# The residual of a layer's last norm in two rounded parts, added by TensorE for seven blocks, and renewals of states spread over more steps

## The chip, the cores and the metric

The kernel runs on one core of one Trainium2 chip. The metric is the device time of one execution in microseconds (us), the median of several runs. Every time in this document comes from such runs or from the hardware profile of one execution. The engines are called PE (TensorE), DVE (VectorE), ACT (ScalarE), POOL (GpSimd) and SP (SyncE, which here only issues DMAs); each runs its own instructions in the order in which they were written into its queue, and waits on semaphores for the others.

## The reference

One inference step of one decoder layer, for 256 tokens of a prompt and 8 sequences of 8 sampled tokens: 320 tokens, model width 2048, all in f32. Cut to what matters here:

```python
def conv_ffn(h, conv_state, w_up, conv_w, conv_b, w_down):
    up = h @ w_up
    up, new_conv = causal_depthwise_conv(up, conv_state, conv_w, conv_b)
    g, u = jnp.split(up, 2, axis=-1)
    return (jax.nn.gelu(g, approximate=True) * u) @ w_down, new_conv

def decoder_layer(x, ssm_state, ssm_conv_state, ffn_conv_state, p):
    ...
    mix = jnp.concatenate([gate_out, ssm_out], axis=-1) @ p["w_out"]
    x = x + rms_norm(mix, p["norm_mix_post"])
    f, new_ffn_conv = conv_ffn(rms_norm(x, p["norm_ffn_pre"]), ffn_conv_state, ...)
    x = x + rms_norm(f, p["norm_ffn_post"])
    return x, new_ssm, new_ssm_conv, new_ffn_conv, chunk_v
```

`ssm_out` comes from a state-space recurrence. Its state of each sampled sequence, 4 groups of heads by 8 sequences, is carried forward: new state = old state times a total decay + (inputs times decays) @ B. The kernel calls this a renewal. It returns the new states, and `y`, the last `x`.

## The kernel before

Everything is kept transposed: the 2048 channels are 16 blocks of 128 partitions, and a block's free axis holds the 320 tokens. Weights are the stationary operand, 128x128; the tokens move, 128x320. To keep f32's accuracy at a faster rate, each f32 operand is split in two parts of the format f32r (a rounded f32): x = hi + lo. A product is three matmuls: hi·hi, hi·lo, lo·hi.

**Slabs.** Weights come in slabs of 512 KB, eight 128x128 blocks (`slab`, from L119): SP loads `wraw`, ACT casts it to `whi` (L130), DVE subtracts to get `wlo` (L132). There are three buffers of each. `accumulate` (L143 to L145) issues the three matmuls of a block, so a slab is 24 of them. All slabs' instructions have a raised priority in the scheduler that writes each engine's order.

**Projections.** `project` runs an up-projection for 512 output columns in 8 slabs: six that hold two input blocks for all four output blocks (input blocks 0 to 11), then two that hold the input blocks 12 to 15 for two output blocks each. `chunk_out` runs one chunk of a down-projection in 8 slabs; DVE adds each result to `acc` (L236). After each slab, `tick` lets a background task of the list `bg` take one step.

**FFN.** 11 groups of 512 columns of each half. `ffn_up(g)` runs two `project` calls (the gate's half, then the other half) from `hT[0]`, `hT[1]` (the two parts of the normed input), with the convolution, GELU and product behind them; `split` (L370 ACT, L371 DVE) makes two parts of the product. `chunk_out` of group g is written after `ffn_up(g + 1)`.

**Renewals.** The background task there is `renewals` (first two steps for the prompt's states, then 4 groups of heads by 2 halves of the sequences, eight batches). For a group ACT copies and DVE scales tokens into `xb_parts` (L1191, L1194); for each of the batch's four states POOL multiplies `st` by the decay (L1199), PE makes `up_ps` (L1211), DVE adds it (L1213), ACT stores the state. SP loads states (L1171) and tokens (L1180) between slabs of weights. A step is a `yield`; the task has 105 of them.

**Tail.** After the last chunk: sums of squares over channels on PE (`token_sums`, L284), the reciprocal root on DVE and ACT, and `spread` (L292), which makes of the root a 128x320 tile in PSUM; ACT copies it to `r4s` for POOL, which doesn't read PSUM here. Then for each of the 16 blocks y = acc · root + x1, where x1 is the residual (in the tile `acc_mix`), and a store of y. `hand_over` (L1244) brings x1 into PSUM (`x1p`) by an f32 matmul with the identity, for blocks 0 to 10. Three engines do the blocks:

- `by_pe` (0 to 3): DVE multiplies, PE adds `acc` into the same PSUM tile by an f32 matmul with the identity (L1281), ACT copies the sum out (L1282) and ACT's queue stores it.
- `whole` (4 to 10): DVE multiplies (`timed`, L1271) and adds x1p (L1276); SP's queue stores (L1248).
- `by_pool` (11 to 15): POOL multiplies (L1271) and adds x1 itself (L1288); SP's queue stores.

`after` and `behind` chain each engine's instructions of the tail in the order in which the calls are written.

Of the kernel before, what the change touches and what calls it, by code (L numbers as in the profile page):

```python
# [34 lines left out]
def hybrid_step(  # L35
# [29 lines left out]
    with tc.high_priority(offset=300000):  # L65
        dve.memset(ones, 1.0)

        ps = misc("early")
        for _ in range(EARLY):
            pe.matmul(ps[:, :P], ones, ones, start=True, stop=True)  # L70
    upper = cp.tile([P, P], F32, name="upper")
    later = cp.tile([P, P], F32, name="later")
    bd2 = cp.tile([P, P], F32, name="bd2")
# [3 lines left out]
    bd = bd2[:NS, :NS]  # L77

    def masks():
        make_upper_triangular(nc, upper, 1.0, diag=True)  # L80
        make_lower_triangular(nc, later, 1.0, diag=False)
        pool.memset(bd2, 0.0)
        for op, fill, base in ((ALU.is_gt, 1.0, 1 - TS), (ALU.is_ge, 0.0, 0)):
            pool.affine_select(out=bd2, in_=bd2, pattern=[[-TS, P // TS], [0, TS]], compare_op=op, fill=fill, base=base,
                               channel_multiplier=1)

        d4 = ident.rearrange("p (i r t) -> p i r t", r=4, t=TS)
        dve.tensor_reduce(out=low[:, 0:1], in_=d4[:, :, 2:4], axis=mybir.AxisListType.XYZ, op=ALU.add)
        d5 = ident.rearrange("p (i k t) -> p i k t", k=2, t=TS)
        dve.tensor_reduce(out=low[:, 1:2], in_=d5[:, :, 1], axis=mybir.AxisListType.XY, op=ALU.add)  # L90
        dve.tensor_scalar(out=low, in0=low, scalar1=-1.0, scalar2=None, op0=ALU.mult)
        for r in range(2):
            rs = slice(64 * r, 64 * r + 64)
            dve.tensor_tensor(out=upper_s[rs], in0=upper[rs, rs], in1=bd2[rs, rs], op=ALU.mult)
        pool.memset(cmask, 1.0)
        cm4 = cmask.rearrange("p (h b) i -> p h b i", h=2)
        pool.affine_select(out=cm4, in_=cm4, pattern=[[0, 2], [-8, 4], [1, 32]],
                           compare_op=ALU.is_ge, fill=0.0, base=0, channel_multiplier=0)
        pool.affine_select(out=cm4, in_=cm4, pattern=[[0, 2], [8, 4], [-1, 32]],
                           compare_op=ALU.is_ge, fill=0.0, base=7, channel_multiplier=0)  # L100
# [63 lines left out]
    def finish(task):  # L164
        while task in bg:
            tick()
# [896 lines left out]
    with tc.tile_pool(name="fp", bufs=1) as fp:  # L1063
# [91 lines left out]
        def renewals():  # L1155

            raw = hp.tile([P, 4, NT], F32R, tag="ohi", name="xb").bitcast(F32).rearrange("p k n -> p (k n)").rearrange("p (h c) -> p h c", h=2)
            part = hp.tile([P, 4, NT], F32R, tag="olo", name="xb_parts").rearrange("p k n -> p (k n)").rearrange("p (h c) -> p h c", h=2)
            tote = fp.tile([P, NH, NB], F32, name="tote")
            for g, s1, x1d, _ in rest:  # L1160
                yield from repeat(None, 2)
                with tc.issue_after(rsqrt_ins[-1]):
                    dve.tensor_tensor(out=s1, in0=s1, in1=x1d, op=ALU.add)
                act.dma_start(o_ssm_p[g], s1)

            def load(g, h):

                st = [fp.tile([P, 512], F32, tag="st", name="st", bufs=4) if h == 0 else
                      cp.tile([P, 512], F32, tag=("s1", "x1d")[i % 2], name="st", bufs=3) for i in range(4)]
                for i in range(4):  # L1170
                    sp.dma_start(st[i], state_ssm[4 * h + i, g])  # L1171
                return st

            def tokens(g):

                rows = xb_d[g].rearrange("(h i t) c -> i t h c", h=2, i=4)
                for i in range(4):
                    for r in range(4):
                        at = 32 * i + TS * r
                        sp.dma_start(raw[at:at + TS], rows[i])  # L1180

            with tc.issue_after(slab_load[-1]):
                sp.dma_start(tote, tote_d)
                ahead = [load(0, 0)]
            yield
            with tc.issue_after(slab_load[-1]):
                tokens(0)
            for g in range(4):
                h0 = 8 * g
                yield from repeat(None, 3)  # L1190
                act.copy(part, raw)  # L1191
                yield
                for at, m in ((slice(0, 512), 0), (slice(512, 640), 1)):
                    dve.scalar_tensor_tensor(out=part[:, :, at], in0=part[:, :, at].bitcast(F32), scalar=low[:, m:m + 1], in1=raw[:, :, at],  # L1194
                                             op0=ALU.mult, op1=ALU.add)
                for h in range(2):
                    st = ahead.pop(0)
                    for i in range(4):
                        pool.tensor_tensor(out=by_head(st[i]), in0=by_head(st[i]),  # L1199
                                           in1=tote[:, h0:h0 + 8, 4 * h + i:4 * h + i + 1].to_broadcast([P, 8, 64]), op=ALU.mult)  # L1200
                        yield
                    if h == 0:
                        ahead.append(load(g, 1))
                    elif g < 3:
                        ahead.append(load(g + 1, 0))
                        tokens(g + 1)
                    yield from repeat(None, 2)
                    grown = [misc("up_ps") for _ in range(4)]
                    for i in range(4):
                        at = slice(32 * i, 32 * i + 32)  # L1210
                        pe.matmul(grown[i], part[at, h, 512:], part[at, h, :512], start=True, stop=True, tile_position=(32 * i, 0))  # L1211
                    for i in range(4):
                        dve.tensor_tensor(out=st[i], in0=st[i], in1=grown[i], op=ALU.add)  # L1213
                        yield
                        act.dma_start(o_ssm_s[4 * h + i, g], st[i])

        NG = NF // 4
        nxt = ffn_up(0)
        grow = renewals()
        bg.append(grow)  # L1220
        for g in range(NG):
            hi, lo = nxt
            if g < NG - 1:
                nxt = ffn_up(g + 1)
            if g == 0:
                acc = fp.tile([P, KD, NT], F32, name="acc_ffn")
            if g == NG - 1:
                finish(grow)
            chunk_out(ffn_w_down, g, hi, lo, g == 0, last if g == NG - 1 else None)

        act.dma_start(o_fconv_p, ptf)
# [5 lines left out]
        def after(engine):  # L1237
            return tc.issue_after(behind[engine]) if engine in behind else nullcontext()

        def hand_over(*blocks, where=banks):  # L1240
            for nb in blocks:
                x1p[nb] = where[0].tile([P, 512], F32, tag=where[1], name="x1p")[:, :NT]
                with after(pe):
                    behind[pe] = pe.matmul(x1p[nb], ident, x1[:, nb, :], start=True, stop=nb > 3).ins  # L1244

        def stored(queue, k, n):
            with after(queue):
# [3 lines left out]
        with after(pe):  # L1251
            sums = token_sums(sq4, more=True)
        behind[pe] = sums_ins[-1]
        hand_over(0)
        with after(pe):
            sums = token_sums(one[0], sums)
        r = rsqrt_by_root(sums, 1.0 / D)
        behind[pe] = sums_ins[-1]
        hand_over(4, 5)
        with after(pe):  # L1260
            r4 = spread(r)
        behind[pe] = spread_ins[-1]
# [5 lines left out]
        def timed(engine, k, n, root):  # L1268
            f = acc[:, k:k + n, :]
            with after(engine):  # L1270
                behind[engine] = engine.tensor_tensor(out=f, in0=f, in1=root.unsqueeze(1).to_broadcast([P, n, NT]), op=ALU.mult).ins  # L1271

        def whole(k, n):
            timed(dve, k, n, r4)
            for nb in range(k, k + n):
                behind[dve] = dve.tensor_tensor(out=acc[:, nb, :], in0=acc[:, nb, :], in1=x1p[nb], op=ALU.add).ins  # L1276
            stored(sp, k, n)
# [7 lines left out]
        def by_pool(k, n):  # L1285
            timed(pool, k, n, r4s)
            with after(pool):
                behind[pool] = pool.tensor_tensor(out=acc[:, k:k + n, :], in0=acc[:, k:k + n, :], in1=x1[:, k:k + n, :], op=ALU.add).ins  # L1288
            stored(sp, k, n)

        timed(dve, 0, 1, r4)
        hand_over(1)
        by_pe(0)
        whole(4, 2)
        hand_over(6, 7, where=more)
        timed(dve, 1, 1, r4)
        by_pe(1)
        by_pool(12, 2)
        whole(6, 2)
        hand_over(2, 8)  # L1300
        timed(dve, 2, 1, r4)
        by_pe(2)
        hand_over(9, 3)
        timed(dve, 3, 1, r4)
        by_pe(3)
        whole(8, 2)
        by_pool(14, 2)
        hand_over(10)
        whole(10, 1)
        by_pool(11, 1)  # L1310


_OUTS = [
# [81 lines left out]
```

## Time and profile before

| | |
|---|---|
| median of 3 runs | 1760.93 us (1760.37 to 1761.53) |
| profiled execution | 1762.04 us |
| its span in the profile | 1760.3 us |
| outside the span | 1.74 us |
| DMA, whole span | 301.38 MB, mean 171 GB/s |
| renewals in the trace | from 938.08 (first xb_parts) on |
| last projection matmul starts, first of the sums of squares starts | 1743.54 us, 1743.76 us |

How to read it: an engine's busy time is a sum over its instructions, and engines overlap. In rows of groups, the source line and engine stand ahead of operation, output <- inputs, shapes and count; behind the bar stand the busy time in us and the mean of one in ns, then the engine's idle time ahead of these instructions and what ended it. In a timeline, start and duration in us come first, and brackets hold the idle time just before and its releaser. In the chain of waits, each row is a piece of the path that ended last. Matmuls are pipelined: one's recorded duration is longer than the distance to the next.

### The profile page before, as it was taken

The page shows a single profiled execution, that of the slowest core. Times are in us where ns is not written, and L with a number is a line of the kernel's source. Part 1 is how long each engine was busy: PE and PEld are TensorE (multiplying, and loading weights), DVE is VectorE, ACT ScalarE, POOL GpSimd, SP SyncE. Part 2 cuts the span into 40 slices and gives each one's busy share as a digit, 9 for nine tenths or more (in the row PEclk, how much of TensorE's full clock was granted, in tenths as well). Part 3 has the DMA queues.
Part 4 walks back from the last instruction along what each step waited for, and adds up shares of the span by engine and source line. Part 5 has one row for each costly group of instructions (what it writes and reads, how often), then busy time and mean ns, then how long its engine had stood idle before and what let it go on. Part 6 is the DMA issues. An engine that isn't in the chain of part 4 may idle for free.

```text
span 1760.3 us, 31124 instructions
## 1 busy us (share of the span) xinstructions
PE 1751.6 (100%) x12178; PEld 1729.8 (98%) x12178; DVE 1154.1 (66%) x1949; ACT 806.6 (46%) x1172; POOL 272.7 (15%) x588
## 2 busy tenths in 40 slices
PE   9999999999999999999999999999999999999998
PEld 9999999999999999999999999999999999999997
DVE  7449754656767576668966677676657565656575
ACT  7344545333854445545544434343434343333335
POOL 1003200000111101021331212130201010111004
PEclk9999999999999999999999999999999999999999
DMA  7466655456665644554756666756454545454542
GB/s 248 144 167 182 185 151 150 153 155 190 216 206 163 201 145 131 166 161 143 228 169 223 189 217 195 222 185 192 151 153 148 156 148 155 148 155 147 155 151 104
DMA packets 228179, 301.38 MB, mean 171 GB/s; under 512 B 19936, under 2 KB 150848, under 8 KB 227840
## 3 DMA queue, kind: packets, MB, share of 16 engines
q1 hardware_dynamic: 215856, 281.27, 52.4%
q10 hardware_dynamic: 10640, 13.60, 2.2%
q0 software_dynamic: 1536, 4.52, 1.0%
q8 instruction: 96, 1.57, 0.4%
q14 instruction: 51, 0.42, 0.1%
HBM read 283.47 MB, written 15.61 MB: 170 GB/s over the span
## 4 chain that ended last, share of the span: by engine, by line
PE 95%; DVE 2%; DMA 1%; ACT 0%; POOL 0%; issue 0%; SPq 0%; POOLq 0%; DVEq 0%; ACTq 0%
PE ps L143 20%; PE ps L145 20%; PE ps L144 20%; PE pd L143 10%; PE pd L144 10%; PE pd L145 10%; PE y_ps L900 1%; DMA wraw<-in_ffn_w_up 1%; DVE wlo L132 1%; PE yo_ps L848 0%; PE sg L705 0%; PE tsum L284 0%; DVE h_lo L374 0%; DVE acc_mix L1042 0%; DMA vt<-in_xT 0%; ACT whi L130 0%
## 5 line engine op out<-in xcount | busy, mean ns | idle before, releaser
L132 DVE TENSOR_TENSOR wlo<-wraw,whi 128x1024 fp32r<-128x1024 f32 x470 | 582.9, 1241 | 436.9 <-ACT whi L130 434.9
L130 ACT CAST whi<-wraw 128x1024 fp32r<-128x1024 f32 x470 | 492.0, 1047 | 730.3 <-PE ps L144 437.7
L143 PE MATMUL ps<-h_hi,whi 128*128 128x320 f32 x2528 | 782.1, 310 | 0.4 <-ACT whi L130 0.4
L144 PE MATMUL ps<-h_lo,whi 128*128 128x320 f32 x2528 | 779.8, 309 | 0.0
L145 PE MATMUL ps<-h_hi,wlo 128*128 128x320 f32 x2528 | 777.8, 309 | 0.0
L143 PEld LDWEIGHTS ps<-h_hi,whi 128*128 128x128 f32 x2528 | 474.8, 188 | 4.2 <-issue 2.3
L144 PEld LDWEIGHTS ps<-h_lo,whi 128*128 128x128 f32 x2528 | 475.1, 188 | 0.0
L145 PEld LDWEIGHTS ps<-h_hi,wlo 128*128 128x128 f32 x2528 | 474.4, 188 | 0.1
L143 PE MATMUL pd<-fhi,whi 128*128 128x320 f32 x704 | 217.2, 309 | 0.0
L144 PE MATMUL pd<-flo,whi 128*128 128x320 f32 x704 | 217.0, 308 | 0.0
L145 PE MATMUL pd<-fhi,wlo 128*128 128x320 f32 x704 | 216.9, 308 | 0.0
L143 PE MATMUL pd<-ohi,whi 128*128 128x320 f32 x448 | 139.5, 312 | 0.0
L145 PE MATMUL pd<-ohi,wlo 128*128 128x320 f32 x448 | 138.5, 309 | 0.0
L144 PE MATMUL pd<-olo,whi 128*128 128x320 f32 x448 | 138.5, 309 | 0.0
L143 PEld LDWEIGHTS pd<-fhi,whi 128*128 128x128 f32 x704 | 132.2, 188 | 0.7 <-issue 0.7
L144 PEld LDWEIGHTS pd<-flo,whi 128*128 128x128 f32 x704 | 132.2, 188 | 0.2 <-issue 0.2
L145 PEld LDWEIGHTS pd<-fhi,wlo 128*128 128x128 f32 x704 | 132.2, 188 | 0.0
L1099 POOL COPY ptf<-pad 128x2 f32<-128x2 f32 x88 | 24.2, 275 | 508.3 <-DVE pad L1087 507.5
L236 DVE TENSOR_TENSOR acc_ffn<-acc_ffn,pd 128x320 f32<-128x320 f32 x160 | 77.2, 482 | 34.5 <-PE pd L145 33.6
L143 PEld LDWEIGHTS pd<-ohi,whi 128*128 128x128 f32 x448 | 84.0, 188 | 1.4 <-issue 0.7
L144 PEld LDWEIGHTS pd<-olo,whi 128*128 128x128 f32 x448 | 84.1, 188 | 0.2 <-issue 0.2
L145 PEld LDWEIGHTS pd<-ohi,wlo 128*128 128x128 f32 x448 | 84.1, 188 | 0.0
(301 smaller groups left out, 1513.6 us busy)
## 6 DMA issues: line engine op xcount, KB each, us to landing
wraw<-in_ffn_w_up SPq DMA_DIRECT2D x176, 512.0 KB
wraw<-in_w_in SPq DMA_DIRECT2D x142, 512.0 KB
wraw<-in_ffn_w_down SPq DMA_DIRECT2D x88, 512.0 KB
wraw<-in_w_out SPq DMA_DIRECT2D x64, 512.0 KB
st<-in_state_ssm SPq DMA_DIRECT2D x64, 256.0 KB
out_ssm_state_sample<-st ACTq DMA_DIRECT2D x32, 256.0 KB
cs<-dacs_d SPq DMA_DIRECT2D x16, 320.0 KB
xr<-in_xT SPq DMA_DIRECT2D x4, 640.0 KB
```

Of the source, the lines that this page charges most:

```text
L130: act.copy(hi[:, :m], raw[:, :m])
L132: dve.tensor_tensor(out=lo[:, :m], in0=raw[:, :m], in1=hi[:, :m].bitcast(F32), op=ALU.subtract)
L143: pe.matmul(ps, whi, xhi, start=first, stop=False)
L144: pe.matmul(ps, whi, xlo, start=False, stop=False)
L145: newest[0] = pe.matmul(ps, wlo, xhi, start=False, stop=last).ins
L236: dve.tensor_tensor(out=acc[:, nb, :], in0=acc[:, nb, :], in1=ps[:, :NT], op=ALU.add)
L900: pe.matmul(ps[64 * i:64 * i + 64, cols], w(hl), x(hl, m, cpx), tile_position=(0, 64 * i), **flags)
L1099: pool.tensor_copy(ptf[:, k, :], pad[:, 256:258])
```

## The change

Line numbers of the changed kernel are 1 to 19 higher. It does five things:

- Twelve blocks of the residual x1 (0 to 11) are split in two f32r parts, one block a step, as a background task after the renewals. The parts go into `hT[0]` and `hT[1]`, the buffers of the FFN's normed input, each block once the last up-projection has read it for the last time. `finish(grow)` moves one group up, so that the renewals end before.
- `hand_over` makes x1p from these parts with two f32r matmuls (with `ident_r`, an f32r identity that POOL makes among the masks at the kernel's start) in place of one f32 matmul, and for blocks 0 to 11 in place of 0 to 10.
- PE adds seven blocks (0 to 3 and 8, 9, 10) in place of four; DVE adds 4 to 7 and 11; POOL keeps 12 to 15 and gives 11 away. DVE multiplies 2 and 3, 8 and 9, 10 and 11 as pairs.
- So ACT's queue stores seven times and SP's five times, in place of four and seven.
- The renewals take more steps: four before the tokens, twelve in place of three ahead of the first group's parts, and two in place of one behind each of POOL's multiplications: 150 steps.

```diff
+    ident_r = cp.tile([P, P], F32R, name="ident_r")
...
     def masks():
+        pool.tensor_copy(ident_r, ident)
...
                 act.dma_start(o_ssm_p[g], s1)
+            yield from repeat(None, 4)
...
-                yield from repeat(None, 3)
+                yield from repeat(None, 3 if g else 12)
...
                                            in1=tote[:, h0:h0 + 8, 4 * h + i:4 * h + i + 1].to_broadcast([P, 8, 64]), op=ALU.mult)
+                        yield
                         yield
...
+        def x1_parts():
+
+            for nb in range(12):
+                split(hT[0][:, nb, :], hT[1][:, nb, :], x1[:, nb, :])
+                yield
+
...
+            if g == NG - 2:
+                finish(grow)
+                parted = x1_parts()
+                bg.append(parted)
             if g == 0:
                 acc = fp.tile([P, KD, NT], F32, name="acc_ffn")
-            if g == NG - 1:
-                finish(grow)
...
+        added = (0, 1, 2, 3, 8, 9, 10)
...
-                with after(pe):
-                    behind[pe] = pe.matmul(x1p[nb], ident, x1[:, nb, :], start=True, stop=nb > 3).ins
+                for i in range(2):
+                    with after(pe):
+                        behind[pe] = pe.matmul(x1p[nb], ident_r, hT[i][:, nb, :], start=i == 0, stop=i == 1 and nb not in added).ins
...
-        hand_over(0)
+        hand_over(0, 1)
...
         hand_over(4, 5)
+        hand_over(6, where=more)
...
         def whole(k, n):
-            timed(dve, k, n, r4)
+            if n:
+                timed(dve, k, n, r4)
+            n = max(n, 1)
...
         timed(dve, 0, 1, r4)
-        hand_over(1)
         by_pe(0)
         whole(4, 2)
-        hand_over(6, 7, where=more)
+        hand_over(7, where=more)
         timed(dve, 1, 1, r4)
         by_pe(1)
         by_pool(12, 2)
         whole(6, 2)
-        hand_over(2, 8)
-        timed(dve, 2, 1, r4)
+        hand_over(2, 3)
+        timed(dve, 2, 2, r4)
         by_pe(2)
-        hand_over(9, 3)
-        timed(dve, 3, 1, r4)
         by_pe(3)
-        whole(8, 2)
+        hand_over(8, 9)
+        timed(dve, 8, 2, r4)
+        by_pe(8)
+        by_pe(9)
         by_pool(14, 2)
-        hand_over(10)
-        whole(10, 1)
-        by_pool(11, 1)
+        hand_over(10, 11)
+        timed(dve, 10, 2, r4)
+        by_pe(10)
+        whole(11, 0)
```

Where this moves instructions, at three places. The first is VectorE at the first renewal. `wlo` is the low half of a slab, its number the slab's; `xb_parts` is what the renewal's matmuls read. Before:

```order
L132 TENSOR_TENSOR wlo_10398<-wraw_10394,whi_10396 128x1024
L132 TENSOR_TENSOR wlo_10434<-wraw_10430,whi_10432 128x1024
L1194 TENSOR_SCALAR xb_parts_9596<-xb_parts_9596,low_91,xb_9595 128x2x512
L1194 TENSOR_SCALAR xb_parts_9596<-xb_parts_9596,low_91,xb_9595 128x2x128
L132 TENSOR_TENSOR wlo_10469<-wraw_10465,whi_10467 128x1024
```

and PE there, which takes the renewal's four matmuls in the middle of the slab whose high half is `whi_10396`:

```order
L145 MATMUL pd_0_10_10400<-fhi_9299,wlo_10398 128x320
L143 MATMUL pd_0_10_10400<-fhi_9299,whi_10396 128x320
L1211 MATMUL up_ps_10277<-xb_parts_9596 128x512
L1211 MATMUL up_ps_10278<-xb_parts_9596 128x512
L1211 MATMUL up_ps_10279<-xb_parts_9596 128x512
L1211 MATMUL up_ps_10280<-xb_parts_9596 128x512
L144 MATMUL pd_0_10_10400<-flo_9300,whi_10396 128x320
```

VectorE after the change:

```order
L134 TENSOR_TENSOR wlo_10547<-wraw_10543,whi_10545 128x1024
L1197 TENSOR_SCALAR xb_parts_9598<-xb_parts_9598,low_92,xb_9597 128x2x512
L1197 TENSOR_SCALAR xb_parts_9598<-xb_parts_9598,low_92,xb_9597 128x2x128
L134 TENSOR_TENSOR wlo_10578<-wraw_10574,whi_10576 128x1024
L134 TENSOR_TENSOR wlo_10608<-wraw_10604,whi_10606 128x1024
L134 TENSOR_TENSOR wlo_10639<-wraw_10635,whi_10637 128x1024
L134 TENSOR_TENSOR wlo_10669<-wraw_10665,whi_10667 128x1024
L134 TENSOR_TENSOR wlo_10722<-wraw_10718,whi_10720 128x1024
L134 TENSOR_TENSOR wlo_10778<-wraw_10774,whi_10776 128x1024
```

and PE's renewal matmuls, now at the end of the slab of `wlo_10846`, whose low half VectorE makes second after the last of the rows above:

```order
L146 MATMUL ps_6656_3_10773<-h_lo_104,whi_10844 128x320
L147 MATMUL ps_6656_3_10773<-h_hi_103,wlo_10846 128x320
L1215 MATMUL up_ps_10872<-xb_parts_9598 128x512
L1215 MATMUL up_ps_10873<-xb_parts_9598 128x512
L1215 MATMUL up_ps_10874<-xb_parts_9598 128x512
L1215 MATMUL up_ps_10875<-xb_parts_9598 128x512
L145 MATMUL ps_6656_0_10770<-h_hi_103,whi_10883 128x320
```

Before, VectorE made the parts behind the low half of the slab that PE needs next, while PE was already in the slab (`10396`) in which it asks for them; now the parts stand eight low halves ahead of the end of the slab in which PE asks.

The second place is ACT in the second half of the last up-projection, `ffn_up(10)`: `whi` is a slab's high half, `gcv` the gate's convolution, `h_hi` the buffer that takes x1's high part (`acc_mix` holds x1). Before:

```order
L1143 DMA out_ffn_conv_sample<-stg_17761 128x64
L130 COPY whi_18149<-wraw_18147 128x1024
L1101 ACTIVATE gcv_17762<-gcv_17762 128x336 x2
L130 COPY whi_18179<-wraw_18177 128x1024
L130 COPY whi_18209<-wraw_18207 128x1024
L130 COPY whi_18239<-wraw_18237 128x1024
```

After:

```order
L1145 DMA out_ffn_conv_sample<-stg_17763 128x64
L372 COPY h_hi_103<-acc_mix_106 128x320
L132 COPY whi_18151<-wraw_18149 128x1024
L1103 ACTIVATE gcv_17764<-gcv_17764 128x336 x2
L372 COPY h_hi_103<-acc_mix_106 128x320 x2
L132 COPY whi_18181<-wraw_18179 128x1024
L372 COPY h_hi_103<-acc_mix_106 128x320 x2
L132 COPY whi_18211<-wraw_18209 128x1024
```

Twelve copies of x1's blocks stand between the casts of the following slabs, two by two; DVE's subtractions stand likewise between the low halves.

The third place is PE at the end of the kernel. Before:

```order
L1281 MATMUL x1p<-acc_ffn,ident 128x320
L1244 MATMUL x1p<-acc_mix,ident 128x320 x2
L1281 MATMUL x1p<-acc_ffn,ident 128x320
L1244 MATMUL x1p<-acc_mix,ident 128x320 x2
L1281 MATMUL x1p<-acc_ffn,ident 128x320
L1244 MATMUL x1p<-acc_mix,ident 128x320
```

After:

```order
L1299 MATMUL x1p<-acc_ffn,ident 128x320 x2
L1259 MATMUL x1p<-h_hi,ident_r 128x320
L1259 MATMUL x1p<-h_lo,ident_r 128x320
L1259 MATMUL x1p<-h_hi,ident_r 128x320
L1259 MATMUL x1p<-h_lo,ident_r 128x320
L1299 MATMUL x1p<-acc_ffn,ident 128x320 x2
L1259 MATMUL x1p<-h_hi,ident_r 128x320
L1259 MATMUL x1p<-h_lo,ident_r 128x320
L1259 MATMUL x1p<-h_hi,ident_r 128x320
L1259 MATMUL x1p<-h_lo,ident_r 128x320
L1299 MATMUL x1p<-acc_ffn,ident 128x320
```

Before, the last matmul hands a block to DVE; now it adds a block that ACT has still to copy out.

## The prediction

> **What bounds the kernel now.** I began with the page: the span, the busy time of each engine, the chain of work that ended last.
>
> ```profile
> span 1760.3 us, 31124 instructions
> PE 1751.6 (100%) x12178; PEld 1729.8 (98%) x12178; DVE 1154.1 (66%) x1949; ACT 806.6 (46%) x1172; POOL 272.7 (15%) x588
> PE 95%; DVE 2%; DMA 1%; ACT 0%; POOL 0%; issue 0%; SPq 0%; POOLq 0%; DVEq 0%; ACTq 0%
> ```
>
> TensorE is busy for 1751.6 of 1760.3 us and is 95% of the chain. A change that takes no matmul out of the projections can win only in the 8.7 us in which PE is idle, or where PE is busy but nobody should have to wait for it (the tail). All edits but one instruction of GpSimd lie in the FFN, so I cut that stage into windows; the columns are the stretch, its length, busy time and count of PE, PEld, DVE, ACT and POOL, the granted clock, the share of the DMA engines and GB/s.
>
> ```profile
> 853.00:939.00 86.00, 86.00 (x589) 85.99 (x588) 67.81 (x116) 47.00 (x68) 32.66 (x73) 1.00 0.63 199
> 939.00:942.00 3.00, 2.41 (x18) 1.94 (x17) 3.00 (x3) 1.37 (x2) 2.48 (x2) 1.00 0.59 182
> 942.00:1222.00 280.00, 280.00 (x1909) 277.37 (x1908) 185.83 (x293) 111.69 (x135) 57.89 (x118) 1.00 0.64 203
> 1222.00:1648.00 426.00, 426.00 (x2906) 425.57 (x2905) 260.35 (x425) 166.34 (x201) 52.06 (x160) 1.00 0.51 154
> 1648.00:1744.00 96.00, 96.00 (x656) 95.83 (x655) 60.44 (x103) 49.56 (x73) 20.20 (x34) 1.00 0.41 128
> 1744.00:1760.40 16.40, 10.79 (x48) 6.94 (x47) 9.11 (x22) 2.89 (x7) 7.81 (x6) 0.93 0.43 160
> ```
>
> From 853 to 1744 us PE is full at the whole clock except in one stretch of 3 us. A matmul of 128x320 in f32r comes every 426.00/2906 = 0.147 us; nothing can make these 891 us shorter but the one hole, and whatever is put beside them is free until it makes PE wait. So two places are left: the hole at 939 and the last 16.4 us.
>
> **The renewals.** The hole is the first matmul of the first renewal.
>
> ```profile
> 938.08 2.48 DVE L1194 SCALAR_TENSOR_TENSOR xb_parts<-xb_parts,low,xb 128x1024 fp32r<-128x1024 f32 x2 [0.26 <-DMA wraw<-in_ffn_w_up]
> 939.82 0.31 PE L143 MATMUL pd<-fhi,whi 128*128 128x320 f32 x1
> 940.71 0.50 PE L1211 MATMUL up_ps<-xb_parts 32*128 32x512 f32 x4 [0.59 <-DVE xb_parts L1194]
> ```
>
> PE starts a projection matmul at 939.82 and the next thing, up_ps, at 940.71: 0.89 us where 0.147 is the pitch, so 0.74 us are lost, and the bracket says to what: VectorE ends xb_parts at 940.56, 0.15 us before. The first place of the order shown above says why: DVE has the parts behind the low half of a slab that PE needs only one slab later. In the changed order eight further low halves (one for each slab of 24 matmuls, 24 × 0.147 = 3.52 us) stand between the parts and the matmul that reads them: some 28 us of room for a lateness of 0.74 us. I take the whole 0.74 us as won; the bounds are 0 (the parts are late for another reason) and 0.74 (there is no other idle time in these windows). What is spread out keeps its number: as many multiplications, additions and state loads, over 150 steps instead of 105. The loads of states stand on SP's queue between the loads of weights and wait for a state buffer; spreading them gives the store that frees it more slabs, not fewer, and the DMA engines are at 0.51 to 0.64 there. Cost 0.
>
> **The splits.** Twelve times an ACT cast and a DVE subtraction of 128x320 go into the second half of the last up-projection, one or two for each of its slabs (second place of the order). The same forms exist, and the stretch in which they will fall is full on PE only:
>
> ```profile
> L370 ACT CAST fhi<-a x44: 453/460/463, 869.8 to 1702.5; 128x320 fp32r<-128x320 f32 x44
> L371 DVE TENSOR_TENSOR flo<-a,fhi x44: 476/484/764, 870.9 to 1704.2; 128x320 fp32r<-128x320 f32 x44
> 1649.00:1673.00 24.00, 24.00 (x166) 24.00 (x165) 14.37 (x23) 11.01 (x15) 4.09 (x14) 1.00 0.50 153
> L132 DVE TENSOR_TENSOR wlo<-wraw,whi 128x1024 fp32r<-128x1024 f32 x121 | 148.2, 1225 | 138.6 <-ACT whi L130 137.8
> L130 ACT CAST whi<-wraw 128x1024 fp32r<-128x1024 f32 x121 | 126.6, 1047 | 216.8 <-PE ps L144 131.8 <-issue 43.7 <-PE pd L144 36.9
> ```
>
> They add 12 × 0.46 = 5.5 us to ACT's 11.0 of 24 and 12 × 0.484 = 5.8 us to DVE's 14.4: both stay under 24. More than load counts what stands behind them: a split may write its two blocks only when PE has read them for the last time, so ACT waits in it, and the next slab's cast is queued behind, then DVE's low half, then PE. That cast itself waits mostly for PE (131.8 of 216.8 us idle): it needs the buffer of three slabs before, released by the very slab that frees the two blocks. So it starts later by two splits at most, 0.92 us on ACT and 0.97 on DVE, overlapping. From the release to a finished low half it is then 0.92 + 1.05 + 0.48 + 1.23 = 3.7 us, while PE still has two slabs (7.0 us) to do: about 3.3 us of cover remain. I take 0. If the cover were gone, the price would be up to 12 × (0.46 + 0.48) = 11.3 us.
>
> **The tail.** It begins as before: the spread of the root waits for the root, not for the residual matmuls ahead of it, and VectorE's operations up to 1751.7 are the same ones. What differs comes after. These rows carry it (in by-form rows the number behind the bar is busy us, then mean ns):
>
> ```profile
> 1753.09 1.54 POOL acc_ffn L1288
> 1754.63 0.82 POOL acc_ffn L1271
> 1755.49 0.89 POOLq L1391
> 1750.74 1.24 PE L1244 MATMUL x1p<-acc_mix,ident 128*128 128x320 f32 x4
> 1754.47 0.70 PE L1244 MATMUL x1p<-acc_mix,ident 128*128 128x320 f32 x2
> 1751.68 1.61 DVE L1271 TENSOR_TENSOR acc_ffn<-acc_ffn,spread 128x320 f32<-128x320 f32 x3
> L1271 DVE TENSOR_TENSOR acc_ffn<-acc_ffn,spread 128x640 f32<-128x640 f32 x3 | 2.4, 814 | 0.0
> L1276 DVE TENSOR_TENSOR acc_ffn<-acc_ffn,x1p 128x320 f32<-128x320 f32 x7 | 3.1, 484 | 0.8 <-PE x1p L1244 0.5
> 1754.67 0.42 ACT L1282 COPY acc_ffn<-x1p 128x320 f32<-128x320 f32 x1 [1.19 <-PE x1p L1281]
> 1755.13 0.34 ACTq L1248 DMA_DIRECT2D out_y<-acc_ffn  x1
> 1755.52 0.86 POOL L1288 TENSOR_TENSOR acc_ffn<-acc_ffn,acc_mix 128x320 f32<-128x320 f32 x1
> ```
>
> Now the chain ends through POOL, whose last addition is done at 1755.52 + 0.86 = 1756.38 and releases the last store. Block 11 leaves POOL, which then ends at 1754.63. PE takes over. One f32 block is two instructions: 1.24 for two blocks against 0.70 for one gives 0.54 us a block. A block in two f32r parts is 2 × 0.147 = 0.29 (the 0.147 is that of the projections; with f32's speed it would be 1.08, but the rows of the projections are the same form). PE's residual work was 11 × 0.54 + 4 × 0.54 = 8.1 us and becomes 12 × 0.29 + 7 × 0.54 = 7.3, but more of it stands at the end. Step by step: VectorE multiplies blocks 2 and 3 from 1751.68 in 0.81, to 1752.5, then 8, 9 and 10, 11, done by 1754.1. PE adds 2 and 3 (1.08) to 1753.6, hands over 8, 9 (0.59) to 1754.2, adds them (1.08) to 1755.3, hands over 10, 11 (0.59) to 1755.9, adds 10; with 0.70 from start to end, and some 0.1 for starts, it is done at about 1756.7. ACT's copy (0.42) follows, and its store 0.04 later: issued at 1757.15, against 1756.4 before. Block 11, added by DVE in 0.48 from 1756.0, is stored at about 1756.6. The last issue is 0.75 us later.
>
> Does the end follow it? The next rows are windows (columns as above), then the DMA engines in tenths and the GB/s over 1749 to 1761 in 40 slices of 0.3 us.
>
> ```profile
> 1755.00:1758.50 3.50, 0.17 (x1) 0.00 (x0) 0.49 (x1) 0.10 (x1) 1.30 (x2) 0.93 0.89 329
> 1758.50:1760.30 1.80, 0.00 (x0) 0.00 (x0) 0.00 (x0) 0.00 (x0) 0.00 (x0) 0.50 0.01 4
> DMA  0000899930199999999459999999988000000000
> GB/s 0 0 0 0 320 397 410 393 120 0 55 358 397 384 401 384 401 354 360 175 201 397 367 410 358 380 380 342 354 316 307 30 17 0 0 0 0 0 0 0
> 1749.36 0.34 ACTq L1248 DMA_DIRECT2D out_y<-acc_ffn  x1
> ```
>
> From 1755.1 to 1758.3 the engines are full at about 380 GB/s, 0.43 us for a block of 164 KB, and from the last byte to the end of the span pass 2 us. A store issued at 1749.36 moves bytes from 1750.2: 0.85 us. So before, 3.2/0.43 = seven and a half blocks (the rest of 2, then 8, 9, 14, 15, 3, 10 and 11) drained from a backlog, and block 11, which could have begun at 1756.4 + 0.85 = 1757.25, came nearly last in it. In the changed order 2, 3, 14 and 15 are issued by 1754.7, 8 at 1755.4, 9 at 1755.9, 11 at 1756.6 and 10 at 1757.15: the engines are full to 1757.2, take 11 to 1757.9, and 10 from 1758.0 to 1758.45. The end goes from 1758.3 to about 1758.5: +0.2 us. Bounds: -0.4 (3, 14, 15, 8, 9, 11 and 10 from 1755.0 without a gap, 7 × 0.41, end at 1757.9) and +0.75 (the end goes with the last issue).
>
> [...]
>
> **The sum** against the profiled execution, 1762.04 us (1760.3 of span and 1.74 around it): -0.74 for the hole, 0 for splits and the identity's rounding copy (POOL is busy 15%), +0.2 for the tail = 1761.5. The median of the runs shown, 1760.93, is 1.11 below that execution, so the same step gives 1760.4.
>
> **Rivals.** *The end goes with the last issue.* For it: the last store then meets idle engines. Against it: the backlog in the rows. -0.74 + 0.75 = 0: 1760.9. Chance 0.12. *The hole stays* or moves to another renewal. For it: four misc banks and four state buffers stay. Against it: the other seven batches, with the same distances, cost PE nothing in the windows. +0.2 alone: 1761.1. Chance 0.05. *The splits starve PE, slower.* Place: the six slabs of the last up-projection's second half. For it: ACT waits inside a split with casts queued behind, and this order is new. Against it: the cast waits for the same slab. It decides once a split holds a cast longer than the cover of 3.3 us, that is if it waited for a slab later (3.52 us) and the next as well; then each of six slabs costs from 0.9 (both ACT casts) to 1.9 us (the DVE steps too), 5 to 11 us: 1766 to 1772. Chance 0.10. *Faster by more than the rows allow:* the places named can give 0.74 + 0.4 = 1.1 us; more needs a gain in a stage where PE is full, which no row offers. Chance 0.07.
>
> **How the numbers follow.** The forecast has the rest, 0.66. About 0.2% (3.5 us) is what a measurement of this kernel can tell from no change; forecast and the first two rivals lie inside: 0.83. Faster 0.07, slower 0.10, from the last two. The range takes in the bounds: 1760.93 - 1.14 = 1759.8 and 1760.93 + 0.75 = 1761.7 (hole kept), each with the 0.6 us by which runs lie off their median: 1759.1 to 1762.5 with a little room; that holds some 8 in 10.
>
> **What would show it.** Right: no wait at the first up_ps; PE at 24.00 of 24.00 while the splits run; residual matmuls at the 0.147 pitch; POOL done by 1754.7; the last store on ACT's queue 0.7 to 0.8 us later on the tail's clock, bytes ending 0.2 us later. Wrong: a PE wait for whi or wlo among the last six slabs of that up-projection, a new idle time at a later renewal, f32r parts that cost 0.5 us each, or bytes that end 0.7 us later.

## The result, and the profile after

The changed kernel takes 1766.51 us, the median of 6 runs (1765.57 to 1767.33), against 1760.82 us for the kernel before (6 runs): a ratio of 1.003, with a 95% interval of 1.0019 to 1.004. It is slower by 5.7 us where 0.5 us less was forecast. The profiled execution took 1766.99 us with a span of 1765.3 us, 5.0 more than the span of before.

TensorE is still the bound, as the page of the changed kernel says, and it is now idle for 11.0 us instead of 8.7:

```profile
span 1765.3 us, 31147 instructions
PE 1754.3 (99%) x12186; PEld 1732.2 (98%) x12186; DVE 1158.4 (66%) x1958; ACT 814.0 (46%) x1187; POOL 268.0 (15%) x587
```

PE's busy time itself grew by 2.7 us, which points at the clock. The FFN by windows (columns as in the prediction) shows where:

```profile
853.00:894.00 41.00, 41.00 (x282) 41.00 (x281) 33.33 (x66) 23.50 (x33) 16.68 (x38) 1.00 0.75 234
894.00:913.00 19.00, 16.09 (x88) 15.20 (x87) 11.26 (x12) 6.00 (x10) 10.88 (x21) 0.82 0.41 121
913.00:1748.70 835.70, 835.70 (x5697) 832.10 (x5695) 536.87 (x871) 351.91 (x450) 135.10 (x328) 1.00 0.55 168
1748.70:1765.30 16.60, 10.66 (x58) 8.08 (x56) 8.64 (x20) 4.28 (x11) 6.16 (x4) 1.00 0.43 159
```

PE is full from 853 to 894 us and from 913 to the tail: the hole at the first renewal is gone and the splits cost nothing. The loss lies in 19 us, at a place where the kernel before has no wait at all. Its row for the same stretch:

```profile
894.00:913.00 19.00, 19.00 (x132) 19.00 (x131) 10.20 (x14) 8.40 (x12) 2.71 (x9) 1.00 0.59 179
```

After the change PE issues 88 matmuls there and would issue 19/0.147 = 129 at the full clock. The view of waits for 890 to 910 us (who waited for whom: us in total, times, longest) and PE's timeline name the chain:

```profile
ACT whi L132 <- POOL pad L1086: 8.1, 1, 8.1
DVE wlo L134 <- ACT whi L132: 4.7, 2, 4.2
...
PE ps L145 <- ACT whi L132: 2.2, 1, 2.2
```

```profile
903.42 0.31 PE L147 MATMUL ps<-h_hi,wlo 128*128 128x320 f32 x1
905.95 0.64 PE L145 MATMUL ps<-h_hi,whi 128*128 128x320 f32 x1 [2.22 <-ACT whi L132]
906.38 0.47 PE L146 MATMUL ps<-h_lo,whi 128*128 128x320 f32 x1
907.21 0.64 PE L147 MATMUL ps<-h_hi,wlo 128*128 128x320 f32 x1 [0.36 <-DVE wlo L134]
```

TensorE waits for a weight slab's cast, the cast for GpSimd. In ScalarE's timeline one sees what stands between them, in GpSimd's why it is late:

```profile
896.28 0.49 ACT L1103 ACTIVATE gcv<-gcv 128x336 f32<-128x336 f32 x1
904.39 0.34 ACTq L1145 DMA_DIRECT2D out_ffn_conv_sample<-stg  x1
904.85 1.04 ACT L132 CAST whi<-wraw 128x1024 fp32r<-128x1024 f32 x1 [8.09 <-POOL pad L1086]
```

```profile
888.68 1.06 POOL L1202 TENSOR_TENSOR st<-st,tote 128x512 f32<-128x512 f32 x1 [11.25 <-DMA tote<-tote_d]
889.69 0.48 POOL L1100 COPY stg<-pad 128x16 f32<-128x16 f32 x1
890.11 0.18 POOL L1101 COPY ptf<-pad 128x2 f32<-128x2 f32 x1
890.25 5.63 POOL L1202 TENSOR_TENSOR st<-st,tote 128x512 f32<-128x512 f32 x4
895.82 0.48 POOL L1100 COPY stg<-pad 128x16 f32<-128x16 f32 x1
896.24 0.53 POOL L1101 COPY ptf<-pad 128x2 f32<-128x2 f32 x1
896.73 4.62 POOL L1202 TENSOR_TENSOR st<-st,tote 128x512 f32<-128x512 f32 x3
...
904.17 0.19 POOL L1100 COPY stg<-pad 128x16 f32<-128x16 f32 x1
```

ScalarE's next entry after 896.77 is the issue of the store of `stg` (the last rows of the sampled sequences). It waits until GpSimd's fourth copy into `stg`, at 904.36, and the cast stands behind it; the bracket of the cast names only the GpSimd instruction that was last by then. GpSimd's copies stand in its own queue between ten multiplications of states, and the first of these waits 11.25 us for the decays (`tote`). In the kernel before, this burst (there eight of the ten; the other two run at 938.89) is over when the evacuation begins, that is the scaling, convolution and GELU of the finished half of an up-projection:

```profile
876.22 6.63 POOL L1199 TENSOR_TENSOR st<-st,tote 128x512 f32<-128x512 f32 x5 [0.77 <-DMA tote<-tote_d]
...
883.21 5.06 POOL L1199 TENSOR_TENSOR st<-st,tote 128x512 f32<-128x512 f32 x3
889.75 0.18 POOL L1099 COPY ptf<-pad 128x2 f32<-128x2 f32 x1 [1.48 <-DVE pad L1087]
```

There the burst runs from 876.2 to 888.3 and the first copy starts at 889.75. The four added steps ahead of the loads (`repeat(None, 4)`, four slabs of about 3.52 us) move the burst 12.5 us later, onto the evacuation.

The size follows from PE's distance to the kernel before, matmul by matmul. It is 0.74 us ahead at 890 us (0.25 from the first loads, 0.49 from a shorter wait at the sums of squares at 849 us, which varies from profile to profile) and 5.63 behind at 912: 6.37 us lost. Three waits make 3.5 of it: 0.63, 2.53 and 0.83 us between starts, each less 0.15 for the pitch. The first of them is a wait for VectorE (`pad`); the other two are the chain above. The other 2.8 us are the clock, below. Then 0.74 come back at the missing hole, and the projections end 1748.57 - 1743.54 = 5.03 us later than before; this is 0.14 more than these terms give, and isn't traced. The tail adds nothing.

### The profile page after: what moved, and what is told of

It is laid out like the page before. It is cut to its first block, busy times and chain, and to the rows that moved or that the text cites. A ratio compares the mean times of both kernels' runs of the same rounds, so it can differ in the third digit from the quotient of the medians.

```text
span 1765.3 us, 31147 instructions
## 1 busy us (share of the span) xinstructions
PE 1754.3 (99%) x12186; PEld 1732.2 (98%) x12186; DVE 1158.4 (66%) x1958; ACT 814.0 (46%) x1187; POOL 268.0 (15%) x587
## 4 chain that ended last, share of the span: by engine, by line
PE 96%; DVE 2%; ACT 1%; issue 0%; POOL 0%; DMA 0%; SPq 0%; DVEq 0%; ACTq 0%
PE ps L145 20%; PE ps L147 20%; PE ps L146 20%; PE pd L145 10%; PE pd L147 10%; PE pd L146 10%; DVE wlo L134 1%; PE y_ps L902 1%; PE yo_ps L850 0%; PE sg L707 0%; PE tsum L286 0%; ACT whi L132 0%; DMA vt<-in_xT 0%; DVE sq L304 0%; PE vt_ps L592 0%
```

## The experiments

**Without the four steps.** Only the lateness of the loads is taken back; the first group waits four steps more, so that what follows keeps its place.

```diff
-            yield from repeat(None, 4)
...
-                yield from repeat(None, 3 if g else 12)
+                yield from repeat(None, 3 if g else 16)
```

> The change, without the four steps ahead of the loads of the decays and the first states; the first group waits 16 steps in place of 12, so that all behind it stays where it was. Theory P (the first burst of GpSimd's multiplications runs late, into the evacuation of the next up-projection, and ScalarE's store and casts wait behind it): the loads land 12 us earlier, the burst runs from 876 to 889 us as before the change, no wait of TensorE near 904 us, granted clock 1.00 from 895 to 913 us; 1760.2 us, 1759.6 to 1760.9. Rival S (the spreading over 150 steps, or the splits of x1, costs it in itself): 1765 to 1767 us.

Measured: 1760.44 us (11 runs) beside 1761.29 for the kernel before (25 runs), ratio 0.9996 (0.9988 to 1.0005). GpSimd's burst stands ahead of the evacuation again:

```profile
874.38 6.93 POOL L1201 TENSOR_TENSOR st<-st,tote 128x512 f32<-128x512 f32 x5 [0.18 <-DMA st<-in_state_ssm]
...
881.45 4.33 POOL L1201 TENSOR_TENSOR st<-st,tote 128x512 f32<-128x512 f32 x3
888.40 0.18 POOL L1101 COPY ptf<-pad 128x2 f32<-128x2 f32 x1 [2.62 <-DVE pad L1089]
```

TensorE waits neither near 904 us nor at the first renewal. One of the change's edits carries the whole loss.

**The four steps alone**, in the kernel before.

```diff
                 act.dma_start(o_ssm_p[g], s1)
+            yield from repeat(None, 4)
```

> The kernel before, with only the four steps added ahead of the loads. Theory P: the same stall near 904 us and the half clock behind it, 6.4 us lost in all (the lag of the changed kernel goes there from -0.74 to 5.63 us): 1767.2 us, 1765.5 to 1768. Rival S: 1760.8 us, no change, since nothing else is spread and the tail is the old one.

Measured: 1767.04 us (6 runs), ratio 1.0032 (1.0019 to 1.0044). PE's starts are 2.53 us apart at 903.48 and 1.01 at 906.26, where the changed kernel has 2.53 and 0.83. The edit makes the loss by itself.

**The halves of the change.** First its renewals with the tail of before and no splits; then its splits and tail with the renewals of before.

```diff
-                parted = x1_parts()
-                bg.append(parted)
...
-                for i in range(2):
-                    with after(pe):
-                        behind[pe] = pe.matmul(x1p[nb], ident_r, hT[i][:, nb, :], start=i == 0, stop=i == 1 and nb not in added).ins
+                with after(pe):
+                    behind[pe] = pe.matmul(x1p[nb], ident, x1[:, nb, :], start=True, stop=nb > 3).ins
...
```

> The change's renewals alone, with the tail of before and no splits. Theory P: all of the loss is here, and the tail of the change is worth 0 to +0.2 us: 1766.2 to 1766.5 us. Rival T (a part of the loss is in the splits or the new tail): 1760 to 1764 us.

```diff
-            yield from repeat(None, 4)
...
-                yield from repeat(None, 3 if g else 12)
+                yield from repeat(None, 3)
...
-                        yield
                         yield
```

> The change's splits and tail alone, with the renewals' 105 steps of before. Theory P: 1760.8 us plus 0 to 0.2 = 1760.8 to 1761.0, the hole at the first renewal kept; no wait of TensorE while the splits run. Rival T: 1762 to 1766 us.

Measured: the renewals alone 1766.02 us (8 runs), 1.0027 (1.0016 to 1.0037); splits and tail alone 1761.34 us (11 runs), 1.0001 (0.9992 to 1.001). The first lies 0.2 us below what was expected, the second 0.3 above, both less than the intervals. The loss is in the renewals; the tail is worth nothing that can be measured, in either direction.

**The store on GpSimd's queue.** The multiplications stay late, but ScalarE no longer waits for GpSimd's copies.

```diff
-                act.dma_start(o_fconv_s[:, k:k + 4], stg[:, half])
+                pool.dma_start(o_fconv_s[:, k:k + 4], stg[:, half])
```

> The changed kernel with the store of the sampled sequences' last rows (stg) issued from GpSimd's queue, behind GpSimd's own copies, instead of ScalarE's. The multiplications stay late, from 889 to 904 us. Theory H (ScalarE's casts wait only because that store heads its queue until GpSimd has copied): casts run on, no wait of TensorE over 1 us near 904, clock 1.00: 1760 to 1761.5 us. Rival C (VectorE, slowed by GpSimd's multiplications, and the tiles that GpSimd prepares are late in themselves): at least 3 us of the stall stay, 1764 to 1766.5 us.

Measured: 1761.5 us (11 runs) beside 1761.13 (33 runs), ratio 1.0003 (0.9994 to 1.0012). ScalarE's timeline of this kernel:

```profile
896.46 0.49 ACT L1103 ACTIVATE gcv<-gcv 128x336 f32<-128x336 f32 x1
896.85 1.03 ACT L132 CAST whi<-wraw 128x1024 fp32r<-128x1024 f32 x1
```

The cast that stood at 904.85 runs at 896.85, directly behind the GELU, though GpSimd's ten multiplications still run from 888.9 to 907.2 us. So the coupling is ScalarE's queue, not the slower engines: of VectorE, which is busy for 8.61 of the 9 us from 895 to 904, PE waits 0.4 us, at 895. The result lies at the upper edge of what was expected; what the last 0.4 us are isn't resolved at this interval.

**Two steps and eight steps** in place of four.

```diff
-            yield from repeat(None, 4)
+            yield from repeat(None, 2)
```

> The changed kernel with two steps instead of four ahead of the first loads. Theory P: the loads land at about 883 us, ten multiplications run to about 897, GpSimd's copies follow and release ScalarE's store by 899; the cast that TensorE needs by 903.5 is in time: 1760.0 to 1761.0 us. Rival (each step of delay costs alike): half of the 6 us, 1763 to 1764 us.

> The changed kernel with eight steps instead of four ahead of the first loads. Theory P: loads land at about 902 us, the multiplications fall in the gap between two evacuations, 902 to 915 us: no stall, 1760.0 to 1761.0 us. Rival (lateness of the loads costs, and more of it costs more): 1766.5 us or above.

Measured: two steps 1761.31 us, 1.0001 (0.9992 to 1.001); eight steps 1760.84 us, 0.9999 (0.999 to 1.0008), 11 runs each. Two steps lie 0.3 us above what was expected, less than the interval. GpSimd's timelines, of the one and of the other, with ScalarE's store and cast of the first:

```profile
882.12 14.30 POOL L1202 TENSOR_TENSOR st<-st,tote 128x512 f32<-128x512 f32 x10 [5.18 <-DMA tote<-tote_d]
896.36 0.46 POOL L1101 COPY ptf<-pad 128x2 f32<-128x2 f32 x1
```

```profile
902.58 13.20 POOL L1202 TENSOR_TENSOR st<-st,tote 128x512 f32<-128x512 f32 x10 [5.27 <-DMA tote<-tote_d]
917.26 0.19 POOL L1101 COPY ptf<-pad 128x2 f32<-128x2 f32 x1 [1.48 <-DVE pad L1089]
```

```profile
899.99 0.34 ACTq L1145 DMA_DIRECT2D out_ffn_conv_sample<-stg  x1
900.45 1.05 ACT L132 CAST whi<-wraw 128x1024 fp32r<-128x1024 f32 x1 [4.44 <-POOL pad L1087]
```

With eight steps the burst lies between two evacuations. With two, it overlaps the evacuation by some 7 us, ScalarE stands still for 4.44 us, and still the cast ends at 901.5, some 1 us ahead of need (TensorE asked for it at 903.42 + 0.15 = 903.57 in the changed kernel, whose GELU there ran 0.76 us later than this one's). The loss doesn't grow with the delay: 0, 2 and 8 steps cost nothing that can be measured, 4 cost 6 us. It is a matter of where the burst falls.

**A shorter tail.** The version without the four steps, with blocks 10 and 11 added by VectorE and handed over early.

```diff
-        added = (0, 1, 2, 3, 8, 9, 10)
+        added = (0, 1, 2, 3, 8, 9)
...
-        hand_over(2, 3)
+        hand_over(2, 3, 8, 9)
+        hand_over(10, 11, where=more)
...
-        hand_over(8, 9)
...
-        hand_over(10, 11)
-        timed(dve, 10, 2, r4)
-        by_pe(10)
-        whole(11, 0)
+        whole(10, 2)
```

> The version without the four steps, and in the tail blocks 10 and 11 are added by VectorE; the residual of 8 to 11 is handed over ahead of the addition of 2, while TensorE waits for VectorE there. Theory: the last issue comes 1.5 us earlier, the DMA engines' rate then sets the end; 0.4 to 0.8 us below the version without the four steps, 1759.7 to 1760.0 us. Rival (the end is set by the rate already): no change, 1760.4 us.

Measured: 1760.74 us (11 runs), 0.9997 (0.9988 to 1.0006) to the kernel before; the version without the four steps had 0.9996. No gain: the 0.4 to 0.8 us expected did not come, and the rival holds. In the profiles the last store is issued at 1754.17 us instead of 1755.26, 1.1 us earlier where 1.5 was expected, but the last bytes move in the same slice of 0.3 us, and both spans are 1758.4 us. First the version without the four steps, then this one (GB/s, 1748 to 1760 us):

```profile
GB/s 0 273 380 405 393 188 0 4 337 393 401 401 384 367 393 77 329 192 60 393 375 380 388 333 346 371 346 363 350 120 0 0 0 0 0 0 0 0 0 0
```

```profile
GB/s 0 213 380 414 401 231 0 0 282 376 384 410 384 401 410 86 311 235 4 367 367 380 393 337 384 410 371 350 350 111 0 0 0 0 0 0 0 0 0 0
```

## Why the prediction was wrong

Point by point:

- *TensorE bounds; 853 to 1744 us are full but for one hole.* Right. That is also why a new wait there is paid in full.
- *The hole goes, 0.74 us.* Right. In the changed kernel the first `up_ps` at 994 us follows its neighbour without a wait, and PE is full from 913 us on.
- *The splits cost 0.* Right: they ran from 1667.5 to 1688.2 us, later than the window taken for them, with PE full. The rival that they starve PE fell, though it named 1766 to 1772 us and the time lies there: right in kind (ScalarE's queue held up ahead of the casts), wrong in place, so that its range was met by luck. Splits and tail alone measure 1.0001.
- *The tail, +0.2 us.* The mechanism held. The span grew by 5.0 us, and the projections end 5.03 later, so the tail took 0.0 more. The last issue, 1762.17 us, is 1757.14 on the clock of before, where 1757.15 was worked out: 0.75 us later than before without moving the end. The forecast's 2 us from the last byte to the end run from the end of the full rate; some bytes trail behind it. The rows in slices of 0.1 us, from 1757 us before and from 1762.03, the same moment, after, show that the full rate lasts some 0.4 us longer and the last bytes move at about 1758.8 in both. The forecast had left out this trail of the kernel before:

```profile
GB/s 346 320 371 333 371 358 333 269 320 358 346 397 180 39 26 26 26 26 0 0 0 0 0 0 0 0 0 0 0 0 0 0 0 0 0 0 0 0 0 0
```

```profile
GB/s 371 320 384 320 371 346 384 320 333 384 384 371 295 384 371 384 205 39 0 0 0 0 0 0 0 0 0 0 0 0 0 0 0 0 0 0 0 0 0 0
```

The shorter tail shows the same from the other side. By the prediction's first rival the end would have moved with the last issue. Here, with a backlog of stores from ScalarE's and SP's queues, it didn't: the last issue came 0.75 us later in the changed kernel and 1.1 us earlier in the shorter tail, and the last bytes moved at about the same time.
- *The renewals' spreading, cost 0.* This step failed. It said that what is spread out keeps its number, and weighed SP's queue and the DMA engines. The later start of the loads also puts ten GpSimd instructions of 1.06 to 2.05 us among GpSimd's copies for the evacuation, where eight of them stood ahead of these copies before. A store on ScalarE's queue waits for those copies, and the casts wait behind the store: 5.7 us on the kernel, where the term was 0. The prediction looked at the order of VectorE, PE and ScalarE; of GpSimd it used only the 15% of busy time, for the identity's copy. What it built on helped to hide this. The table of the profile before dates the renewals from 938.08, the first `xb_parts`, but GpSimd multiplies states from 876.22 on; and the list of changes puts the four steps "before the tokens", though they stand ahead of the loads of the decays and of the first states too. In the kernel before the burst ends 1.5 us ahead of the first copy; that row would have shown how little room there was for a move of four slabs.

Without that edit the rest of the change measures what was forecast for the whole, 0.9996 with the forecast at 0.9997; this doesn't stand out from no change, nor does any version beat the kernel before beyond its interval. That the clock's part is 2.8 us is read from the profile, not tried by an experiment of its own; the times of the single runs, in the last section, fit it.

## What to carry to other kernels

When background work is delayed or spread, its count says nothing: look on each in-order queue at what it will stand in front of at its new time, and follow from there who waits on that queue. Here a store in ScalarE's queue held up the cast behind it for 8.09 us, until its producer, GpSimd, was done; issued from GpSimd's queue it let the cast run at 896.85 instead of 904.85. So put such a DMA on the producer's queue, or where nothing urgent follows. A lightly loaded engine (GpSimd is 15% busy) stood at the head of the critical path here, and whether it did changed with the phase: two and eight steps cost nothing that could be measured (1.0001 and 0.9999), four cost 5.7 us.

## What the runs showed of the hardware

**The clock falls after a stall, in some executions.** The changed kernel's windows show the granted clock (the third number from the end) at 0.71 and then 0.50 behind the wait, with 9 matmuls in 2 us in place of 14; below it the renewals alone, with the same 2.53 us between starts at 903.19 and the clock at 1.00 throughout:

```profile
904.00:908.00 4.00, 1.69 (x5) 1.29 (x6) 1.60 (x2) 3.15 (x5) 0.88 (x9) 0.71 0.04 8
908.00:910.00 2.00, 2.00 (x9) 2.00 (x8) 1.98 (x2) 0.54 (x1) 0.00 (x0) 0.50 0.85 242
910.00:912.00 2.00, 2.00 (x9) 2.00 (x9) 0.00 (x0) 0.00 (x0) 0.00 (x0) 0.50 0.87 242
```

```profile
904.00:908.00 4.00, 1.58 (x9) 1.32 (x10) 1.83 (x2) 3.38 (x5) 0.65 (x7) 1.00 0.04 9
908.00:910.00 2.00, 2.00 (x15) 2.00 (x15) 1.75 (x2) 0.32 (x1) 0.00 (x0) 1.00 0.92 281
```

So waits of 3.5 us cost 6.4 us in one execution, and waits of 3.7 us about 4.0 in the other, and the runs of the second kernel scatter from 1764.54 to 1767.6 us. Over the 20 runs of the three kernels with this stall (the changed one, the four steps alone, the renewals alone) the granted clock goes with the time: the four runs at 1.000 took 1764.54 to 1765.07 us, the four at 0.997 took 1767.12 to 1768.12.

The traces also show what goes with the difference. The half clock lasts 6.83 us, twice 3.413, in the changed kernel and 3.41 in the kernel before with the four steps. The whole clock of the changed kernel lasts whole multiples of 3.413 us: 901.12 us (264 of them) ahead of the stall and 853.33 us (250) behind it. The next rows are cut at these boundaries: the changed kernel ahead of the fall and at half clock, the kernel before with the four steps likewise, and the renewals alone, with boundaries counted back in such steps from the fall of its clock after its last matmuls, at 1761.83.

```profile
902.30:905.71 3.41, 1.43 (x10) 1.16 (x8) 0.00 (x0) 0.86 (x1) 2.58 (x12) 1.00 0.04 10
905.72:912.54 6.82, 6.23 (x22) 5.83 (x23) 3.59 (x3) 2.82 (x5) 0.00 (x0) 0.50 0.57 166
```

```profile
903.58:906.99 3.41, 0.77 (x4) 0.30 (x2) 1.00 (x1) 2.08 (x4) 1.36 (x9) 1.00 0.04 10
907.00:910.40 3.40, 3.13 (x12) 3.13 (x13) 2.58 (x3) 1.61 (x2) 0.00 (x0) 0.50 0.55 169
```

```profile
901.67:905.08 3.41, 1.83 (x13) 1.57 (x11) 0.00 (x0) 0.46 (x1) 2.98 (x12) 1.00 0.01 3
905.08:908.49 3.41, 2.07 (x12) 1.81 (x13) 2.32 (x2) 3.24 (x5) 0.00 (x0) 1.00 0.15 26
```

The clock fell after a stretch with PE busy for 1.43 or 0.77 of 3.41 us, and stayed after stretches with 1.83 and 2.07, where a boundary cuts the wait in two. These are three executions. That the busy time of such a stretch decides is a reading of them that no run tests, and where between 1.43 and 1.83 a line would lie, no run shows.

**VectorE's steps take longer beside GpSimd's multiplications.** In VectorE's timeline a convolution step (`L1096` before, `L1098` after, 128x336) takes 0.52 us alone and 1.3 beside a multiplication of states. First the kernel before, then the changed one:

```profile
893.18 1.04 DVE L1096 SCALAR_TENSOR_TENSOR gcv<-pad,prm,gcv 128x336 f32<-128x336 f32 x2
```

```profile
897.78 3.93 DVE L1098 SCALAR_TENSOR_TENSOR gcv<-pad,prm,gcv 128x336 f32<-128x336 f32 x3
```

The multiplication takes 1.06 us or up to 2.05; that the convolution steps lengthen it isn't shown. In the run with the store on GpSimd's queue, TensorE's only wait there was the one of 0.4 us.
